# Hybrid delta-rule and retention block on one core: a pause in the background copies and additions of block sums

## The chip, the cores and the metric

The kernel runs on one core of a Trainium2 chip. The metric is the device time of one execution in microseconds (us); of several runs the median counts. The engines of the core are TensorE (PE in the profile, PEld its weight loads), VectorE (DVE), ScalarE (ACT), GpSimd (POOL) and SyncE (SP); each works through its own queue in order. DMA transfers are issued from the queues of SP, ACT and POOL and share the core's 16 DMA engines.

## The reference

One block of a network on 512 rows of 1024 numbers, all in float32:

```python
xn = rmsnorm(x, n_mix_pre)
proj = xn @ w_in                                   # 1024 x 14352, split into q, k, v, z, gates ...
oa = chunk_gated_delta_rule(qa, ka, va, beta, g)   # first branch: 8 heads
ya = (rmsnorm(oa, norm_a) * silu(za)) @ w_br_a
ob = chunk_retention(rotary(qb), rotary(kb), vb)   # second branch: 4 heads
yb = (rmsnorm(ob, norm_b) * silu(gb)) @ w_br_b
mix = (sigmoid(gate_a) * ya + sigmoid(gate_b) * yb) @ w_out
x = x + rmsnorm(mix, n_mix_post)                   # output projection and its norm
hn = rmsnorm(x, n_mlp_pre)
ff = square(relu(hn @ w_up)) @ w_down              # MLP, 4096 wide
return x + rmsnorm(ff, n_mlp_post)
```

## The kernel before

**Products.** Every float32 product is made of three matmuls: operands are split into a high and a low part, and high x high, high x low and low x high are summed in PSUM. Weights come in blocks of 512 KB into a buffer `raw` (L102; two buffers of the pool `ring`, and at most times two more of a second pool, taken in turn); `split_weights` then makes the high part on ScalarE (L145, `whi`, or `keep` where it is to stay) and the low part on VectorE (L146, `wlo`). SyncE's queue issues these loads.

**Block sums.** Several large products use Strassen's scheme with seven instead of eight products of blocks. They need sums of weight blocks, which depend on the weights alone. Class `BlockSums` makes them in device memory, in the background: a sum is made in a tensor `sums`, first by a copy of one block (`copy_block`, two halves of 512 KB, SyncE's queue, L166) and then by additions of other blocks to it, done by the DMA itself (`add_block`, GpSimd's queue, L132). Ten such sets are made: one for z, one for each of the two gates, four for the values and gates of the retention heads, and three for the first three groups of `w_down`. That is 56 copies and 56 additions, 112 jobs. Some additions take another sum as their source (`sums<-sums`) and wait for its landing. The last two sets are those of the second and third group of `w_down`: in the order rows below their tensors are `sums_95` to `sums_98` and `sums_99` to `sums_102`.

**What sets when a job is issued.** `pace` is called behind every load of weights. It has a reckoned time, `spent`: in the first phase that of a planner's clock, later a count that every product advances by its number of columns. When `spent` has reached `queued`, one job is issued behind that load, an addition where its copies are done and the last job was a copy, else a copy, and `queued` grows by `JOB_US`. `queued` starts at `JOBS_FROM`. With 65 and 8.0 the last of the 112 jobs falls due at 65 + 111 * 8 = 953. When a product wants a sum whose jobs are still open, they are all issued at once. The scheduler that orders the instructions of each queue may then move loads among the jobs, but additions keep their program order.

**The stages.** First phase: projections and the delta rule, with chains of small work between the products. Second phase: four retention heads, each a unit of scores, values and gates, and at the end a unit for the second gate (`gate_unit(gb_sums, ...)`), the last unit. Then the last part of `w_br_b` and the mixing of both branches (L1656 to L1666), which ends with transposes into `mix`. After that the pools of the phases are closed and the pool `pm` takes over their memory. Output projection: `row_tiles` with `w_out`, in row tiles of 128 rows; tiles 2 and 3 share the weight blocks as they come, then tile 0, then tile 1, from the kept weights. Each has two PSUM banks of the four named `mm`, so tile 0 takes those of tile 2. After a tile, `mix_done` norms it: `add_normed` squares both halves on ScalarE (L1718) and multiplies them by the broadcast row `post` (`norm_mix_post`) on VectorE (L1729, which also is the last reader of the banks), takes the root (L408 on ScalarE), adds to the residual in `acc` (L1734), norms again with the row `wmlp` (L1759), and TensorE transposes the result (L394) into `hn`. The residual, four loads of x into `acc` (L1738), and the rows `post` and `wmlp` (L1676) are issued on GpSimd's queue, the same as the additions. The next norm's row, `norm_mlp_post`, takes the buffer of `post` when the last tile has used it. Then the MLP: four groups of a product with `w_up` (L92 to L94) and one with `w_down`, the first three by Strassen's scheme (L314) with the block sums.

Of the kernel before, what the change touches and what calls it, by code (L numbers as in the profile page):

```python
# [25 lines left out]
OFF_BA = 6144  # L26
OFF_QB, OFF_KB, OFF_VB, OFF_GB = 6160, 7184, 8208, 10256
OFF_GA, OFF_GBR = 12304, 13328
JOBS_FROM, JOB_US = 65.0, 8.0
SMALL_US, CONV_US, TOK_US, PK_US, INV_US, DB_US = 10.5, 6.5, 2.5, 2.0, 46, 1.2  # L30
VT_US, KS_US, PX_US, PC_US, GATE_US, FEAT_US, INV_PRIO, CONV_PRIO, SMALL_PRIO, KEY_PRIO, DECAY_US, AHEAD, TR_US, REC_PRIO, OUT_PRIO, SUM_PRIO = 2.5, 2.4, 3.5, 2.4, 11.0, 1.0, 0, 600, 800, 600, 20.0, 700, 2.2, 900, 900, 300
DFF = 4096


def shape_constants():
# [27 lines left out]
def hybrid_block_kernel(ctx: ExitStack, tc: tile.TileContext, a: dict, out: bass.AP):  # L63
# [11 lines left out]
    added, spent, queued, clocks = [False], [None], [JOBS_FROM], []  # L75
# [20 lines left out]
    def weights(src, k0, nk, c0, ncols, keep=None, paced=True):  # L96

        n = nk * ncols
        i = next(loads)
        pool, tag = raw_pools[i % len(raw_pools)]  # L100
        raw = pool.tile([P, 1024], F32, tag=tag, name="raw", bufs=2)
        load = nc.sync.dma_start(  # L102
            raw[:, :n].rearrange("p (k c) -> p k c", k=nk),
            src[k0 * P : (k0 + nk) * P, c0 : c0 + ncols].rearrange("(k p) c -> p k c", p=P),
        )
        pace(load)
        with ExitStack() as behind:
            for mark in marks if i < 9 else ():
                behind.enter_context(tc.issue_after(mark.ins))
            return split_weights(raw, n, nk, keep, ahead[0] if i >= 6 else 0)  # L110

    def pace(load):

        if clocks:
            spent[0] = clocks[0].now
        if spent[0] is None:
            return
        if spent[0] < queued[0] or not (trickle or later_adds):
            return
        queued[0] += JOB_US  # L120
        with tc.issue_after(load.ins):
            ready = bool(later_adds) and not any(job[0] is later_adds[0][2] for job in trickle)
            if ready and (added[0] or not trickle):
                add_block()
                added[0] = False
            else:
                copy_block()
                added[0] = True

    def add_block():  # L130
        dst, src, _ = later_adds.pop(0)
        tc.keep_in_program_order(nc.gpsimd.dma_start(dst, src, accum_op=ALU.add))  # L132

    def copy_block():
        sums, part, k = trickle.pop(0)
        sums.copy(part, k)
# [53 lines left out]
    def block_raw(block):  # L190
        n = next(loads)
        pool, tag = raw_pools[n % len(raw_pools)]
        raw = pool.tile([P, 1024], F32, tag=tag, name="raw", bufs=2)
        load = nc.sync.dma_start(raw.rearrange("p (k c) -> p k c", k=2), block)
        pace(load)
        return raw
# [1753 lines left out]
```

## Time and profile before

| | |
|---|---|
| median of 3 runs | 1349.22 us (1349.13, 1349.22, 1353.59) |
| the profiled execution | 1350.82 us, span from first to last instruction 1349.0 us |
| mean granted TensorE clock | 0.996 of full |
| busy: PE, PEld, DVE, ACT, POOL | 98%, 81%, 69%, 47%, 6% of the span |
| DMA | 210.57 MB, 156 GB/s in the mean |

| stretch, us | PE busy | granted clock | DMA share |
|---|---|---|---|
| 0 to 200 | 195.53 | 1.00 | 0.59 |
| 200 to 400 | 197.83 | 1.00 | 0.61 |
| 400 to 600 | 198.47 | 1.00 | 0.71 |
| 600 to 800 | 199.80 | 1.00 | 0.64 |
| 800 to 900 | 99.38 | 1.00 | 0.39 |
| 900 to 950 | 49.22 | 1.00 | 0.68 |
| 950 to 1000 | 43.47 | 0.93 | 0.58 |
| 1000 to 1100 | 99.64 | 1.00 | 0.56 |
| 1100 to 1300 | 200.00 | 1.00 | 0.42 |
| 1300 to 1349 | 41.49 | 0.97 | 0.20 |

The second table is the view of stages, with the four rows from 1000 to 1100 taken together: the busy time of TensorE in each stretch, the share of full speed that its clock was granted, and the mean busy share of the 16 DMA engines. The first phase ends at about 500 us, the second at about 955, the output projection at about 1005, where the products with `w_up` begin. In a row of a timeline the first number is the start in us from the span's beginning, the second the duration, then engine, line, operation, output and input; the brackets hold the idle time before and what ended it. A row of waits reads: who waited, for whom, us in total, how many times, the longest.

### The profile page before, as it was taken

To read this page: it belongs to the slowest core of one execution; us is meant where nothing else is said; L and a number is where in the kernel's file an instruction comes from. 1 tells how busy PE (TensorE), PEld (TensorE's weight loads), DVE (VectorE), ACT (ScalarE), POOL (GpSimd) and SP (SyncE) were. 2 spreads that over 40 slices of the span, in tenths; PEclk is the share of its full clock that TensorE was granted. 3 is DMA by queue.
4 is the path that set the end of the run, shared out by engine and by line. 5 is a ranking of instruction groups with operands and counts; after the bars stand their busy time and mean duration, and the time that the engine had idled before them with its cause. 6 is when DMAs were issued, how large, how long until landed. Compare 5 with 4: busy or idle time off the path is not lost.

```text
span 1349.0 us, 17489 instructions
## 1 busy us (share of the span) xinstructions
PE 1324.8 (98%) x6615; PEld 1097.6 (81%) x6615; DVE 935.2 (69%) x1575; ACT 638.0 (47%) x1126; POOL 79.8 (6%) x83
## 2 busy tenths in 40 slices
PE   9999999999999999999999999999899999999997
PEld 7888888887888878888888888878689888888886
DVE  6889867486566578886676776889475745828535
ACT  5783336554534524544443443445255746346441
POOL 2201100011000001000000000000110000000000
PEclk9999999999999999999999999999999999999999
DMA  6338943467775477886483661656926443625421
GB/s 194 132 105 184 212 105 78 110 166 199 212 163 130 114 198 166 284 252 161 115 230 93 183 193 48 202 161 187 235 85 193 161 151 109 187 95 177 134 79 63
DMA packets 105701, 210.57 MB, mean 156 GB/s; under 512 B 6598, under 2 KB 30320, under 8 KB 105104
## 3 DMA queue, kind: packets, MB, share of 16 engines
q1 hardware_dynamic: 88592, 167.27, 39.2%
q0 software_dynamic: 14704, 35.30, 15.7%
q10 hardware_dynamic: 2320, 6.89, 1.4%
q8 instruction: 52, 0.85, 0.3%
q14 instruction: 33, 0.27, 0.1%
HBM read 205.21 MB, written 62.93 MB: 199 GB/s over the span
## 4 chain that ended last, share of the span: by engine, by line
PE 78%; DVE 8%; DMA 6%; ACT 5%; issue 2%; POOL 0%; DVEq 0%; ACTq 0%; POOLq 0%
PE mm L665 17%; PE mm L314 12%; PE mm L92 10%; PE mm L93 10%; PE mm L94 10%; PE dl L314 9%; PE dl L665 5%; DVE wlo L146 2%; DMA raw<-in_w_in_dram 2%; DMA raw<-sums 1%; DMA post<-in_norm_mix_post_dram 1%; PE tr L674 1%; PE dl L93 1%; ACT whi L145 1%; PE dl L94 1%
## 5 line engine op out<-in xcount | busy, mean ns | idle before, releaser
L145 ACT CAST whi<-raw 128x1024 fp32r<-128x1024 f32 x259 | 272.0, 1052 | 408.9 <-PE mm L93 96.4
L146 DVE TENSOR_TENSOR wlo<-raw,whi 128x1024 fp32r<-128x1024 f32 x259 | 315.4, 1221 | 213.6 <-ACT whi L145 212.3
L665 PE MATMUL mm<-actT,whi 128*128 128x512 f32 x448 | 144.3, 403 | 0.0
L314 PE MATMUL mm<-whi,xsum 128*128 128x512 f32 x384 | 120.5, 390 | 0.0
L94 PE MATMUL mm<-hn,wlo 128*128 128x512 f32 (+1 forms) x288 | 105.4, 366 | 0.0
L93 PE MATMUL mm<-hn,whi 128*128 128x512 f32 (+1 forms) x288 | 105.3, 366 | 0.0
L92 PE MATMUL mm<-hn,whi 128*128 128x512 f32 (+1 forms) x288 | 105.3, 366 | 0.0
L665 PEld LDWEIGHTS mm<-actT,whi 128*128 128x128 f32 x448 | 80.5, 188 | 14.9
L665 PE MATMUL mm<-actT,wlo 128*128 128x512 f32 x224 | 87.7, 392 | 0.0
L314 PEld LDWEIGHTS mm<-whi,xsum 128*128 128x128 f32 x384 | 72.0, 188 | 14.8
L314 PE MATMUL mm<-wlo,xsum 128*128 128x512 f32 x192 | 75.1, 391 | 0.4 <-DVE wlo L146 0.4
L665 PE MATMUL mm<-whi,og 128*128 128x512 f32 x192 | 62.4, 397 | 0.0
L94 PEld LDWEIGHTS mm<-hn,wlo 128*128 128x128 f32 x288 | 54.3, 189 | 8.8
L665 PE MATMUL mm<-whi,actT 128*128 128x512 f32 x176 | 60.4, 405 | 1.0 <-DVE qf L903 1.0
L93 PEld LDWEIGHTS mm<-hn,whi 128*128 128x128 f32 x288 | 54.3, 189 | 8.7
L92 PEld LDWEIGHTS mm<-hn,whi 128*128 128x128 f32 x288 | 54.3, 189 | 8.7
L314 PE MATMUL dl<-whi,ffq 128*128 128x512 f32 x192 | 61.1, 389 | 0.0
L314 PE MATMUL dl<-whi,actT 128*128 128x512 f32 x192 | 61.1, 389 | 0.0
L1782 DVE TENSOR_TENSOR ffq<-r,ffq 128x512 fp32r<-128x512 f32 (+2 forms) x51 | 33.7, 677 | 29.1 <-ACT ffq L1782 29.0
L132 POOL DMA_DIRECT2D sums<-in_w_in_dram x28 | 32.5, 1162 | 355.2 <-DMA sums<-in_w_in_dram 355.2
L92 PE MATMUL mm<-actT,whi 128*128 128x512 f32 x128 | 51.5, 403 | 0.0
L94 PE MATMUL mm<-actT,wlo 128*128 128x512 f32 x128 | 50.8, 397 | 0.0
(394 smaller groups left out, 2894.7 us busy)
## 6 DMA issues: line engine op xcount, KB each, us to landing
raw<-in_w_in_dram SPq DMA_DIRECT2D x95, 512.0 KB, 4.9
raw<-sums SPq DMA_DIRECT2D x56, 512.0 KB, 4.0
raw<-in_w_up_dram SPq DMA_DIRECT2D x36, 512.0 KB, 4.2
sums<-in_w_in_dram SPq DMA_DIRECT2D x32, 512.0 KB, 5.9
sums<-in_w_in_dram POOLq DMA_DIRECT2D x28, 512.0 KB, 7.3
raw<-in_w_down_dram SPq DMA_DIRECT2D x26, 512.0 KB, 3.8
sums<-in_w_down_dram SPq DMA_DIRECT2D x24, 512.0 KB, 6.3
sums<-sums POOLq DMA_DIRECT2D x16, 512.0 KB, 7.9
```

The costliest lines, as they stand in the source:

```text
L92: nc.tensor.matmul(ps, lh, rh, start=first, stop=False)
L93: nc.tensor.matmul(ps, lh, rl, start=False, stop=False)
L94: nc.tensor.matmul(ps, ll, rh, start=False, stop=last)
L132: tc.keep_in_program_order(nc.gpsimd.dma_start(dst, src, accum_op=ALU.add))
L145: nc.scalar.copy(hi[:, :n], raw[:, :n])
L146: nc.vector.tensor_tensor(lo[:, :n], raw[:, :n], hi[:, :n], ALU.subtract)
L314: m = nc.tensor.matmul(pss[t], lhs[i // 2], rhs[i % 2], start=first and k + i == 0, stop=k + i == 5, skip_group_check=not first,)
L665: m = tc.keep_in_program_order(nc.tensor.matmul(*args, **kwargs))
L674: tc.keep_in_program_order(nc.tensor.transpose(ps, src, ident if by is None else by))
L1782: return nc.scalar.copy(dst[0], r), nc.vector.tensor_tensor(dst[1], r, dst[0], ALU.subtract)
```

## The change

Two numbers of the planner change and one rule is added: the jobs start at a reckoned 70 instead of 65 us, fall due every 8.5 instead of 8.0 us, and a job that would fall due between a reckoned 860 and 985 us is put off to 985. By this count 93 jobs fall due before the pause (the 93rd at 70 + 92 * 8.5 = 852) and 19 from 985 on, the last at 985 + 18 * 8.5 = 1138.

```diff
-JOBS_FROM, JOB_US = 65.0, 8.0
+JOBS_FROM, JOB_US = 70.0, 8.5
...
+REST = 860.0, 985.0
...
         queued[0] += JOB_US
+        if REST[0] < queued[0] < REST[1]:
+            queued[0] = REST[1]
         with tc.issue_after(load.ins):
```

The change moves instructions on two queues, SyncE's and GpSimd's; on TensorE, VectorE and ScalarE the same operations stand in the same order as before.

GpSimd's queue around the loads of x and of the norms' rows, before (`acc` is the residual, `post` and `wmlp` the norms' rows, `sums_95` and up the sums for the second and third group of `w_down`):

```order
L132 DMA sums_98<-in_w_down_dram 128x2x512 x2
L1738 DMA acc_624<-in_x_dram 128x1024 x2
L132 DMA sums_99<-in_w_down_dram 128x2x512
L1738 DMA acc_624<-in_x_dram 128x1024
L132 DMA sums_100<-sums_99 128x1024
L132 DMA sums_101<-sums_100 128x1024
L132 DMA sums_99<-in_w_down_dram 128x2x512
L1738 DMA acc_624<-in_x_dram 128x1024
L1676 DMA post_8155<-in_norm_mix_post_dram 128x1024
L1676 DMA wmlp_8157<-in_norm_mlp_pre_dram 128x1024
L132 DMA sums_100<-sums_99 128x1024
L1676 DMA post_8616<-in_norm_mlp_post_dram 128x1024
```

The same place with the change:

```order
L135 DMA sums_97<-sums_96 128x1024
L1741 DMA acc_624<-in_x_dram 128x1024 x4
L1679 DMA post_8144<-in_norm_mix_post_dram 128x1024
L1679 DMA wmlp_8146<-in_norm_mlp_pre_dram 128x1024
L1679 DMA post_8600<-in_norm_mlp_post_dram 128x1024
L135 DMA sums_95<-in_w_down_dram 128x2x512
L135 DMA sums_96<-sums_95 128x1024
L135 DMA sums_97<-sums_96 128x1024
L135 DMA sums_98<-in_w_down_dram 128x2x512 x2
L135 DMA sums_99<-in_w_down_dram 128x2x512
L135 DMA sums_100<-sums_99 128x1024
L135 DMA sums_101<-sums_100 128x1024
```

Between the first load of x and the second row there were four additions and are now none; 13 additions, five of which stood ahead of the first load of x, now follow the third row.

SyncE's queue from the last unit of the second phase to the MLP, before (`raw` are weight loads, `sums<-in_w_down_dram` the copies):

```order
L194 DMA raw<-sums 128x1024
L166 DMA sums<-in_w_down_dram 128x2x512
L194 DMA raw<-in_w_in_dram 128x2x512
L194 DMA raw<-sums 128x1024
L194 DMA raw<-in_w_in_dram 128x2x512
L102 DMA raw<-in_w_br_b_dram 128x1024
L166 DMA sums<-in_w_down_dram 128x2x512
L102 DMA raw<-in_w_br_b_dram 128x1024 x3
L102 DMA raw<-in_w_out_dram 128x1024 x8
L102 DMA raw<-in_w_up_dram 128x2x512 x12
L102 DMA raw<-in_w_down_dram 128x2x512 x2
```

And with the change:

```order
L197 DMA raw<-sums 128x1024
L197 DMA raw<-in_w_in_dram 128x2x512
L103 DMA raw<-in_w_br_b_dram 128x1024 x4
L103 DMA raw<-in_w_out_dram 128x1024 x8
L103 DMA raw<-in_w_up_dram 128x2x512 x11
L169 DMA sums<-in_w_down_dram 128x2x512
L103 DMA raw<-in_w_up_dram 128x2x512
L103 DMA raw<-in_w_down_dram 128x2x512 x2
L169 DMA sums<-in_w_down_dram 128x2x512
L197 DMA raw<-sums 128x1024 x2
```

The copies ended with the loads of `w_br_b` before; now the last six of them, those of the third group's sums except its first tensor, stand among the loads of `w_up` and `w_down` of the first two groups of the MLP.

## Prediction

> **What bounds the kernel now.** The page comes first: TensorE is busy for 98% of the span, so a change that only moves background transfers can give at most the 24 us in which TensorE is not busy, and only where it waits for one of them.
>
> ```profile
> span 1349.0 us, 17489 instructions
> PE 1324.8 (98%) x6615; PEld 1097.6 (81%) x6615; DVE 935.2 (69%) x1575; ACT 638.0 (47%) x1126; POOL 79.8 (6%) x83
> ```
>
> The view of waits for TensorE over the whole run, longest first, then tells where that is. One wait stands far above all others:
>
> ```profile
> PE mm L92 <- DVE nh_v L1720: 6.5, 1, 6.5
> PE warm L472 <- DVE warm L461: 1.2, 1, 1.2
> ```
>
> It happens once, in the output projection (L92 is the matmul helper, L1720 is in the norm that follows each row tile). The table by stages puts it between 970 and 980 us, with TensorE busy for 3.47 us of 10 and DMA engines full (share 1.03), and shows a granted clock of 0.79 in the ten microseconds behind it:
>
> ```profile
> 970.00:980.00 10.00, 3.47 (x14) 2.56 (x13) 1.32 (x4) 2.66 (x5) 0.87 (x1) 0.87 1.03 326
> 980.00:990.00 10.00, 10.00 (x37) 8.00 (x36) 7.04 (x25) 3.26 (x11) 0.00 (x0) 0.79 0.15 33
> ```
>
> The timeline of TensorE there gives the size (start, duration; in brackets the idle time and what ended it):
>
> ```profile
> 970.01 0.39 PE L92 MATMUL mm<-keep,actT 128*128 128x512 f32 x1
> ...
> 972.50 0.39 PE L94 MATMUL mm<-keep,actT 128*128 128x512 f32 x1
> 979.42 0.79 PE L92 MATMUL mm<-whi,actT 128*128 128x512 f32 x1 [6.53 <-DVE nh_v L1720]
> ...
> 984.24 0.39 PE L94 MATMUL mm<-keep,actT 128*128 128x512 f32 x1
> ```
>
> The matmul at 979.42 is the first of row tile 0. It needs a PSUM bank that still holds row tile 2, and VectorE had not read that bank, because its first reader multiplies by the row `post`, which was not there:
>
> ```profile
> 978.68 0.69 DVE L1729 TENSOR_TENSOR fw<-mm,post 128x512 f32<-128x512 f32 x1 [12.98 <-DMA post<-in_norm_mix_post_dram]
> ```
>
> The cause lies one queue further back. GpSimd's queue is in order, and the load of `post` stands in it behind additions of block sums, which wait for one another's landing:
>
> ```profile
> 951.59 0.87 POOL L132 DMA_DIRECT2D sums<-sums  x1 [4.44 <-DMA sums<-in_w_down_dram]
> 960.52 0.82 POOL L132 DMA_DIRECT2D sums<-sums  x1 [8.07 <-DMA sums<-sums]
> 961.78 1.35 POOL L1738 DMA_DIRECT2D acc<-in_x_dram  x1
> 962.40 1.28 POOL L1676 DMA_DIRECT2D post<-in_norm_mix_post_dram  x1
> ...
> 1007.34 0.55 POOL L1676 DMA_DIRECT2D post<-in_norm_mlp_post_dram  x1 [31.56 <-DVE nr_y L413]
> ```
>
> The last of the four loads of x into `acc` goes out at 961.78 and `post` at 962.40, with no wait of their own noted: the queue had only just let them through. And it landed late, since the additions were still moving; the table of DMA issues has the microseconds from issue to landing at the end of each row:
>
> ```profile
> acc<-in_x_dram POOLq DMA_DIRECT2D x4, 512.0 KB, 5.1
> post<-in_norm_mix_post_dram POOLq DMA_DIRECT2D x1, 512.0 KB, 16.2
> wmlp<-in_norm_mlp_pre_dram POOLq DMA_DIRECT2D x1, 512.0 KB, 17.5
> post<-in_norm_mlp_post_dram POOLq DMA_DIRECT2D x1, 512.0 KB, 6.7
> ```
>
> 962.40 + 16.2 = 978.6, which is where VectorE starts.
>
> **The change, part by part.** First, the rest. On GpSimd the four loads into `acc` and the two rows now follow one another with no addition between them (rows in the section on the change); TensorE, VectorE and ScalarE keep their order. What `post` then waits for are the release of `acc` and of the memory that the closed pools held, whose last users the timeline shows:
>
> ```profile
> 953.90 0.68 DVE L1659 SCALAR_TENSOR_TENSOR tb<-tb,acc 128x512 f32<-128x512 f32 x1
> 955.45 0.63 PE L394 MATMUL tr<-cmat,tb 128*128 128x128 f32 x4
> ```
>
> So it goes out at about 955.45 + 0.63 = 956.1 instead of 962.4. VectorE's read takes 0.74 us to release TensorE (978.68 to 979.42), and TensorE wants the bank at 972.50 + 0.23 = 972.73; `post` is in time if it lands by 972.0, within 15.9 us of its issue. The nearest row is the same kind of load in the next norm, 6.7 us, and gives 962.8; the slow one, 16.2 us, would give 972.3 and 0.3 us of wait. I take the 6.7, because the 16.2 belongs to a stretch in which additions filled the engines, and none are left there. The wait ends.
>
> What it is worth: start to start, TensorE loses 979.42 - 972.50 - 0.23 = 6.69 us. Then it runs slow: from 979.42 to 984.24 lie 11 matmuls in 4.82 us, and 11 of the same form take 970.01 to 972.50 = 2.49 us at full clock, so 2.33 us more. Together 9.02 us. The Trainium skill ("TensorE: Matmul & The Clock Gate", Part 1: The HAM clock gate) says that the clock is halved after an idle window of about 3.4 us and comes back after about 3.4 us of work; by it the slow part would cost an estimated 1.7 us instead of 2.33, and the trace agrees in kind, with twice the spacing after 6.5 us of idleness.
>
> What of that is given back. The norm chain could not use its whole lead. ScalarE loads its table for the square root behind the squares, under the wait until now; without the wait this is on the chain:
>
> ```profile
> 972.34 1.28 ACT L408 ACT_TABLE_LOAD   x1
> 980.12 0.20 ACT L408 ACTIVATE nr_y<-nh_v 128x1 f32<-128x1 f32 x1 [6.51 <-DVE nh_v L1721]
> 986.11 1.42 DVE L1759 SCALAR_TENSOR_TENSOR fw<-acc,nr_y,wmlp 128x512 f32<-128x512 f32 x2
> 989.95 0.60 PE L394 MATMUL tr<-cmat,fw 128*128 128x128 f32 x4
> ```
>
> The root moves from 980.12 to the table's end at 973.62, 6.5 us earlier, and the normed row is ready at 986.11 + 1.42 - 6.5 = 981.0. TensorE's transposes of it move by 9.02, from 989.95 to 980.9; the first four need only the first half of the row. That is just met, and as the later tiles follow the same chain with a few tenths of slack, I give back 0.3 us. 9.02 - 0.3 = **8.7 us gained**.
>
> Second, the 19 jobs that come later: 6 copies on SyncE's queue and 13 additions on GpSimd's, 8 of which stood in this stretch before, 5 ahead of it. In the first feature product of the MLP a weight block lasts 24 matmuls, and the stage rows show 44 matmuls in 5 us, so 2.7 us a block:
>
> ```profile
> 1010.00:1015.00 5.00, 5.00 (x44) 5.00 (x43) 4.55 (x8) 3.36 (x8) 1.13 (x1) 1.00 0.87 204
> 1020.00:1025.00 5.00, 5.00 (x44) 5.00 (x44) 2.45 (x2) 2.64 (x4) 0.00 (x0) 1.00 1.06 329
> 1008.43 2.70 POOL L132 DMA_DIRECT2D sums<-in_w_down_dram  x2
> q1 hardware_dynamic: 88592, 167.27, 39.2%
> q0 software_dynamic: 14704, 35.30, 15.7%
> ```
>
> By the two queue rows 512 KB occupy all engines for 0.392 * 1349 * 0.524 / 167.27 = 1.66 us as a load and 0.157 * 1349 * 0.524 / 35.30 = 3.14 us on GpSimd's queue. The additions start behind the MLP's `post`, at 1007.34 - 8.7 = 998.6, and the first three wait for one another, so in the 22 us of the eight blocks fall some 3 * 3.14 + 8 * 1.66 = 22.7 us of traffic: full, but before, too, the row at 1007.34 and two additions at 1008.43 ran beside these blocks, with shares of 0.87 to 1.06, and TensorE was busy 5.00 us of 5. So I take 0. From above: the next four additions (12.6 us of engine time) come in a burst at about 1018; were the loads held up that long, the four raw buffers (two pools of two) still cover 4 * 2.7 = 10.9 us of it at best and nothing at worst, so 1.7 to 12.6 us. The Trainium skill ("DMA: Bandwidth & Descriptors", Queues, rings and completion order) has the engines take turns between queue rows by packets, so that additions slow the loads that run beside them; that speaks against the change, and the rows above say that it has not yet cost TensorE anything.
>
> Are the sums late? The second group's first block sum was fetched at 1115.14, the third group's at 1196.74:
>
> ```profile
> 1115.14 5.58 SPq L194 DMA_DIRECT2D raw<-sums  x2
> 1196.74 5.58 SPq L194 DMA_DIRECT2D raw<-sums  x2
> 1077.08 21.90 SPq L102 DMA_DIRECT2D raw<-in_w_up_dram  x8
> sums<-in_w_down_dram POOLq DMA_DIRECT2D x12, 512.0 KB, 11.2
> raw<-in_w_up_dram SPq DMA_DIRECT2D x36, 512.0 KB, 4.2
> ```
>
> Less 8.7 these are 1106 and 1188. Three chained additions of 11.2 us from 998.6 end at 1032; the last of the third group go out behind copies that stand between the eight weight loads of 1077 to 1099, and end before 1130. Both have over 50 us in hand: cost 0.
>
> Third, the interval. Up to the rest, 93 jobs run at 8.5 instead of 8.0 us of reckoned time, and every sum is still copied long before its use. TensorE is idle for 5.6 us of these 795:
>
> ```profile
> 65.00:860.00 795.00, 789.42 (x4023) 652.56 (x4022) 579.00 (x1014) 362.29 (x658) 55.43 (x52) 1.00 0.62 160
> ```
>
> That is the most that it could give. A copy can as well fall ahead of another load than before; for a loss I bound it by the same 5.6 us, and take 0, as the longest waits there are for VectorE and ScalarE.
>
> The sum: the profiled execution took 1350.82 us for a span of 1349.0; it becomes 1340.3 of span and 1342.1. The median of the runs is 1349.22, so 1349.22 - 8.7 = **1340.5 us**.
>
> **Rivals.** *The row is still late.* With the 17.5 us of `wmlp` from 956.1, `post` lands at 973.6, 1.6 us too late; the wait stays too short to bring back the slow clock, if the rule above holds, and 1342.1 comes out. For it: weight loads share the engines at that time. Against it: the four loads into `acc` on the same queue took 5.1 us in the median. Chance 0.10.
>
> *Crowding in the MLP.* The burst of additions eats half of the buffers' lead: 12.6 - 5.4 = 7.2 us at most, about 4 in the middle, 1344.5. For it: shares of 1.06 already. Against it: TensorE's full stages beside them. Chance 0.16.
>
> *Starved loads, slower.* At the start of the second half of the first group, about 1018, loads find no buffer lead and TensorE stops for the whole 12.6 us, in two pieces that each bring the slow clock, 2 * 2.33 more: 17.3 - 8.7 = 8.6 us slower, 1357.8. It decides if loads of `w_up` take longer than 10.9 us to land. Against it: 4.2 us is their median now. Chance 0.05.
>
> *No effect.* Another transfer lets VectorE go at the same time, or the rest is filled otherwise: 1349. But ScalarE's squares were done when its table load began at 972.34, the loads into `acc` are ahead of `post`, and the order shows the rest to be empty. Chance 0.04.
>
> **How the numbers follow.** The forecast keeps 0.65, with a range of its own of 1338.5 to 1343. A measurement of this kernel can tell about 0.5%, here 6.7 us, from no change; faster means under 1342.5. The forecast gives 0.61 of that and the late row 0.06, crowding 0.05: 0.72. Slower is the starved case and a little of the interval's unknown: 0.06. The rest, 0.22, is no change. For 8 in 10 the range reaches over the late row and the middle of crowding: 1338.5 to 1346.5.
>
> **What would show it.** In the profile of the changed kernel `post` goes out near 956 and lands before 972; the wait of L92 for L1720 is gone; the granted clock reads 1.00 from 950 to 1000; the table load stands between the squares and the root; additions stand at 999 and later, and TensorE is full from 1000 to 1100. Idle time of L92 to L94 for `whi` or `wlo` after 1000, or `post` landing after 972, would make the prediction wrong, as would new waits of over 3 us before 940.

## The result and the profile after

| | before | after |
|---|---|---|
| median of 5 runs each, us | 1349.91 (1349.13 to 1353.59) | 1340.97 (1338.08 to 1342.55) |
| span of the profiled execution, us | 1349.0 | 1339.2 |
| first matmul of the output projection starts at, us | 950.27 | 949.27 |
| from there to the end of the span, us | 398.7 | 389.9 |

The ratio of the times is 0.9924, 95% interval 0.9904 to 0.9945: faster by 0.55% to 0.96%. The last row of the table is the difference of the two rows above it. It will serve as the yardstick of the experiments, because what lies ahead of the projection varies between executions of the same code: in five profiles in which the program is the changed kernel up to there, the first matmul of the projection starts between 946.2 and 950.6 us. The yardstick is not exact either: a second profile of the changed kernel has 391.0 instead of 389.9, so differences of about 1 us in it say little. Every distance, landing and wait below comes from one profiled execution of its kernel.

The code has moved by three lines: L92 to L94 are now L93 to L95, L394 is L397, L1729 is L1732. The busy line of the page of after:

```profile
span 1339.2 us, 17492 instructions
PE 1323.0 (99%) x6615; PEld 1095.8 (82%) x6615; DVE 935.8 (70%) x1575; ACT 637.6 (48%) x1126; POOL 78.1 (6%) x83
```

TensorE does as many matmuls in about the same busy time (1324.8 before). The span lost 9.8 us: 8.0 of idle time and 1.8 of busy time, since a slow matmul counts as busy. In the view of waits of after, TensorE alone, from 940 us to the end, the row of 6.5 us is gone and one row is left:

```profile
PE tr L397 <- DVE fw L1762: 0.3, 1, 0.3
```

The table by stages of after, for the places that the prediction named:

```profile
970.00:980.00 10.00, 10.00 (x47) 8.23 (x46) 7.14 (x23) 5.79 (x16) 0.00 (x0) 1.00 0.00 0
980.00:990.00 10.00, 10.00 (x54) 8.47 (x53) 8.34 (x27) 5.58 (x15) 0.00 (x0) 1.00 0.00 0
...
1060.00:1080.00 20.00, 20.00 (x89) 16.30 (x88) 12.96 (x15) 8.77 (x11) 0.85 (x1) 1.00 1.03 258
```

From 970 to 990 TensorE is full at a granted clock of 1.00, and the DMA engines, full from 970 to 980 before, have nothing to do. The traffic went to the MLP: in the last row they are full (1.03), in this profile without a loss on TensorE. GpSimd's timeline of after:

```profile
945.56 0.53 POOL L1741 DMA_DIRECT2D acc<-in_x_dram  x1 [4.17 <-DVE tb L1662]
953.88 0.53 POOL L1741 DMA_DIRECT2D acc<-in_x_dram  x1 [7.79 <-DVE tb L1662]
955.63 0.53 POOL L1679 DMA_DIRECT2D post<-in_norm_mix_post_dram  x1 [1.23 <-DMA raw<-in_w_out_dram]
...
997.27 0.53 POOL L1679 DMA_DIRECT2D post<-in_norm_mlp_post_dram  x1 [40.59 <-DVE nr_y L416]
997.79 1.25 POOL L135 DMA_DIRECT2D sums<-in_w_down_dram  x1
```

Between the last loads of x and the rows no addition stands (the first two loads, at 936.02 and 940.85, have none behind them either), and the brackets name what ended each wait: VectorE's last reads of the old memory, and for `post` a load of `w_out`. `post` leaves at 955.63 instead of 962.40. The table of DMA issues of after:

```profile
post<-in_norm_mix_post_dram POOLq DMA_DIRECT2D x1, 512.0 KB, 8.3
...
raw<-in_w_up_dram SPq DMA_DIRECT2D x36, 512.0 KB, 5.3
```

It lands at 955.63 + 8.3 = 963.9. So VectorE's first read of the bank waits for something else now, the squares on ScalarE (timeline of VectorE, then of ScalarE):

```profile
970.59 0.69 DVE L1732 TENSOR_TENSOR fw<-mm,post 128x512 f32<-128x512 f32 x1 [7.88 <-ACT junk L1721]
```

```profile
971.32 1.28 ACT L411 ACT_TABLE_LOAD   x1
972.61 0.20 ACT L411 ACTIVATE nr_y<-nh_v 128x1 f32<-128x1 f32 x1
```

and TensorE goes from tile 2 and 3 to tile 0 without a gap (timeline of TensorE):

```profile
971.48 0.39 PE L95 MATMUL mm<-keep,actT 128*128 128x512 f32 x1
971.71 0.39 PE L93 MATMUL mm<-whi,actT 128*128 128x512 f32 x1
...
974.20 0.39 PE L95 MATMUL mm<-keep,actT 128*128 128x512 f32 x1
...
979.88 0.60 PE L397 MATMUL tr<-cmat,fw 128*128 128x128 f32 x4
```

These are the last matmul of the two tiles, the first and the twelfth of tile 0, and the transposes of the normed row. Before they stood at 972.50, 979.42, 984.24 and 989.95.

### The profile page after: what moved, and what is told of

Its sections match the earlier page's. It is cut to its first block, busy times and chain, and to the rows that moved or that the text cites. A ratio compares the mean times of both kernels' runs of the same rounds, so it can differ in the third digit from the quotient of the medians.

```text
span 1339.2 us, 17492 instructions
## 1 busy us (share of the span) xinstructions
PE 1323.0 (99%) x6615; PEld 1095.8 (82%) x6615; DVE 935.8 (70%) x1575; ACT 637.6 (48%) x1126; POOL 78.1 (6%) x83
## 4 chain that ended last, share of the span: by engine, by line
PE 83%; DVE 7%; ACT 5%; DMA 4%; issue 1%; DVEq 0%; ACTq 0%; SPq 0%
PE mm L668 17%; PE mm L317 12%; PE mm L95 11%; PE mm L94 11%; PE mm L93 11%; PE dl L317 8%; PE dl L668 5%; DVE wlo L149 2%; DMA raw<-in_w_in_dram 2%; PE dl L93 1%; PE dl L95 1%; PE dl L94 1%; DMA raw<-sums 1%; PE tr L397 1%; PE tr L677 1%
## 5 line engine op out<-in xcount | busy, mean ns | idle before, releaser
L95 PE MATMUL mm<-hn,wlo 128*128 128x512 f32 (+1 forms) x288 | 105.4, 366 | 0.0
L94 PE MATMUL mm<-hn,whi 128*128 128x512 f32 (+1 forms) x288 | 105.3, 366 | 0.0
L93 PE MATMUL mm<-hn,whi 128*128 128x512 f32 (+1 forms) x288 | 105.3, 366 | 0.0
L95 PEld LDWEIGHTS mm<-hn,wlo 128*128 128x128 f32 x288 | 54.3, 189 | 8.8
L94 PEld LDWEIGHTS mm<-hn,whi 128*128 128x128 f32 x288 | 54.3, 189 | 8.7
L93 PEld LDWEIGHTS mm<-hn,whi 128*128 128x128 f32 x288 | 54.3, 189 | 8.7
L93 PE MATMUL mm<-actT,whi 128*128 128x512 f32 x128 | 51.5, 403 | 0.0
L95 PE MATMUL mm<-actT,wlo 128*128 128x512 f32 x128 | 50.8, 397 | 0.0
```

Source lines behind the costliest of these rows:

```text
L93: nc.tensor.matmul(ps, lh, rh, start=first, stop=False)
L94: nc.tensor.matmul(ps, lh, rl, start=False, stop=False)
L95: nc.tensor.matmul(ps, ll, rh, start=False, stop=last)
```

## Experiments

Each experiment starts from the kernel before or from the changed one, as its diff shows. "Distance" is the last row of the table above: from the first matmul of the output projection to the end (398.7 us before, 389.9 after).

**Pause or interval?** The change has two parts that can both move the additions. First the numbers alone, without the pause:

```diff
-JOBS_FROM, JOB_US = 65.0, 8.0
+JOBS_FROM, JOB_US = 70.0, 8.5
```

> Jobs from 70 every 8.5, without the pause. In GpSimd's queue the row post then stands behind only two additions that come after the first load of x (one onto sums_97, one onto sums_98), and neither has to wait for another's landing, since their sources were finished long before. Theory 1 (the row stood behind additions that wait for one another): post goes out by 957, lands before 971, the wait of tile 0 for its bank is gone, and the time is 8 to 9 us below the kernel before, ratio 0.993 to 0.995, although there is no pause. Theory 2 (the pause, that is less traffic around the output projection, brings the gain): post lands after 975, TensorE still waits 5 to 7 us, ratio 0.999 to 1.001.

Measured: 1340.0 us (1338.69 to 1341.81, 5 runs), ratio 0.9932, interval 0.9915 to 0.995; distance 389.9. GpSimd's timeline of this kernel shows how:

```profile
943.45 0.90 POOL L132 DMA_DIRECT2D sums<-sums  x1
944.01 1.54 POOL L132 DMA_DIRECT2D sums<-in_w_down_dram  x1
946.61 0.58 POOL L1738 DMA_DIRECT2D acc<-in_x_dram  x1 [1.06 <-DVE tb L1659]
...
956.49 0.53 POOL L1676 DMA_DIRECT2D post<-in_norm_mix_post_dram  x1 [3.93 <-PE tr L394]
```

Two additions still stand among the loads of x, but neither waits for another's landing, and nothing is held up; `post` lands 8.3 us after its issue. Then the pause alone, with 65 and 8.0:

```diff
+REST = 860.0, 985.0
...
+        if REST[0] < queued[0] < REST[1]:
+            queued[0] = REST[1]
```

> The pause alone, jobs from 65 every 8.0. No addition stands between the loads of x and the rows. Theory 1 and theory 2 both: the wait for post is gone, ratio 0.993 to 0.995. Theory 3 (part of the gain comes from the longer interval in the first two phases): 1 to 3 us less gain than the whole change, ratio 0.995 to 0.997, and TensorE reaches the output projection about 1 us later than with the whole change.

Measured: 1340.49 us (1338.18 to 1342.98, 6 runs), ratio 0.9932, interval 0.9914 to 0.9951; distance 389.7. Either part does the whole work, and the two together (the change, once more beside other kernels) no more than each:

> The changed kernel itself, once more on the chip of the two kernels beside it: 1338 to 1342.5 us, no wait of L95 for the norm. If either of the other two stands below it by more than 2 us in the median, a version without a pause beats it.

Measured: 1339.78 us (1338.28 to 1341.39, 6 runs), ratio 0.9912, interval 0.9894 to 0.9931; distance 391.0. Of the 1.1 us above the first profile's 389.9, TensorE idles 0.7 between 1060 and 1080, where it waits for split weights in the MLP (of which below):

```profile
1060.00:1080.00 20.00, 19.30 (x84) 15.34 (x83) 11.87 (x13) 8.11 (x9) 0.85 (x1) 1.00 0.99 253
```

The times of the three kernels agree. So it is not the pause as such, and not the interval as such: both clear the place ahead of `post` of additions that wait for each other.

**The queue or the traffic?** In the next kernel the additions stay where they were before; only the rows `post` and `wmlp` change their queue, from GpSimd's to SyncE's.

```diff
-        def broadcast_row(vec, tag):
+        def broadcast_row(vec, tag, eng=nc.gpsimd):
...
-            rows_in.append(nc.gpsimd.dma_start(w, vec.partition_broadcast(P)))
+            rows_in.append(eng.dma_start(w, vec.partition_broadcast(P)))
...
-        wpost = broadcast_row(a["norm_mix_post"][0], "post")
-        wmlp = broadcast_row(a["norm_mlp_pre"][0], "wmlp")
+        wpost = broadcast_row(a["norm_mix_post"][0], "post", nc.sync)
+        wmlp = broadcast_row(a["norm_mlp_pre"][0], "wmlp", nc.sync)
```

> The kernel before, with all its jobs where they were, but post and wmlp are loaded from SyncE's queue. Theory 1: post goes out at about 956 and, among the additions' traffic, lands 7 to 16 us later, so between 963 and 972; TensorE waits 0 to 1 us, the clock stays at 1.00 or nearly, ratio 0.993 to 0.996. Theory 2 (traffic): it lands near 978 as before, wait of 5 to 7 us, ratio 0.999 to 1.001.

Measured: 1342.53 us (1339.24 to 1348.93, 12 runs), ratio 0.9951, interval 0.9934 to 0.9967; distance 391.5. SyncE's timeline of this kernel, its DMA issue of `post`, GpSimd's timeline, and its view of waits for TensorE from 940 us:

```profile
955.51 0.33 SPq L1676 DMA_DIRECT2D post<-in_norm_mix_post_dram  x1
...
956.39 0.46 SPq L102 DMA_DIRECT2D raw<-in_w_out_dram  x1
```

```profile
post<-in_norm_mix_post_dram SPq DMA_DIRECT2D x1, 512.0 KB, 8.3
```

```profile
962.77 0.82 POOL L132 DMA_DIRECT2D sums<-sums  x1 [10.03 <-DMA sums<-sums]
```

```profile
PE mm L93 <- DVE keep L146: 0.8, 1, 0.8
PE mm L92 <- ACT keep L145: 0.6, 1, 0.6
```

The row goes out at 955.51, and on GpSimd's queue additions go on at 951.88, 962.77 and 963.32, with the fourth load of x held up until 964.03 as before. The row lands in 8.3 us all the same, and the wait for the norm is gone. The 1.4 us of other waits are the price of the new place: the rows are issued ahead of the last load of `w_out`, whose split TensorE then waits for. So the additions hurt by standing ahead of the row in its queue. The addition of 951.88, which lands only at about 962.7, runs beside the row and does no harm; those of 962.77 and 963.32 go out as the row lands, at 963.8, so what they would do beside it is not shown.

The opposite: a chain put back. With 70 and 9.5 and no pause, the jobs reach the projection later, and a chain of three additions stands ahead of the fourth load of x and of `post`.

```diff
-JOBS_FROM, JOB_US = 65.0, 8.0
+JOBS_FROM, JOB_US = 70.0, 9.5
```

> No pause, jobs from 70 every 9.5, so fewer transfers than in the changed kernel up to the output projection, but by this count three additions that wait for one another (onto sums_95, 96 and 97) stand between the loads of x, ahead of post. Theory 1 (the chain in GpSimd's queue sets the time): the first goes out at about 942, the next two after 8 to 9 us each, the fourth load of x and post at about 961 to 963; post lands 8 to 16 us later, at 969 to 979. TensorE waits 0 to 7 us for the bank, and the time lies between the changed kernel's and that before, ratio 0.994 to 1.000, most likely 0.997. Theory 3 (a longer interval is what helps): ratio 0.993 or lower, as with 8.5.

GpSimd's timeline of this kernel, its DMA issue of `post`, and its waits of TensorE:

```profile
940.80 1.24 POOL L132 DMA_DIRECT2D sums<-in_w_down_dram  x1
...
948.76 0.86 POOL L132 DMA_DIRECT2D sums<-sums  x1 [3.47 <-DMA sums<-in_w_down_dram]
956.65 0.81 POOL L132 DMA_DIRECT2D sums<-sums  x1 [7.03 <-DMA sums<-sums]
957.20 0.84 POOL L1738 DMA_DIRECT2D acc<-in_x_dram  x1
958.10 0.56 POOL L1676 DMA_DIRECT2D post<-in_norm_mix_post_dram  x1
```

```profile
post<-in_norm_mix_post_dram POOLq DMA_DIRECT2D x1, 512.0 KB, 13.2
```

```profile
PE dl L314 <- DVE wlo L146: 1.1, 2, 0.8
PE mm L92 <- DVE nh_v L1720: 1.1, 1, 1.1
PE dl L314 <- ACT whi L145: 0.9, 1, 0.9
```

Measured: 1346.42 us (1341.93 to 1355.88, 12 runs), ratio 0.9976, interval 0.9959 to 0.9994; distance 394.1. The wait for the norm is back, but with 1.1 us: here the chain began earlier, and `post` was held only until 958.10. Still it landed 13.2 us later, against 8.3 without a chain. That gives the lateness of before two parts: in the kernel before `post` was issued 5.8 us later than in the changed one (counted from the first matmul of the projection: 12.13 against 6.36) and took 7.9 us longer to land (16.2 against 8.3). By these numbers neither part alone would have cost much: an estimate for the kernel before is 962.40 + 8.3 = 970.7 with the late issue alone, in time for the 972.0 of the prediction, and 956.6 + 16.2 = 972.8 with the slow landing alone, 0.8 us late. The other 2.0 us of waits in this kernel are in the MLP, of which below.

**A late row without any addition.** If the lateness of the row is all that counts, the changed kernel must fall back when the row is late for another reason. In three kernels GpSimd fills the row's buffer with zeros several times (1 us each) before the load; nothing else is changed, and the extra fills are overwritten. The row `wmlp` now goes out ahead of `post`, behind the first fill.

```diff
-        def broadcast_row(vec, tag):
+        def broadcast_row(vec, tag, fills=0):
...
+            for _ in range(fills):
+                nc.gpsimd.memset(w, 0.0)
...
-        wpost = broadcast_row(a["norm_mix_post"][0], "post")
+        wpost = broadcast_row(a["norm_mix_post"][0], "post", 15)
```

Fifteen fills:

> The changed kernel, but GpSimd first fills the buffer of post 15 times, about 0.95 us each, so that the row goes out at about 970 instead of 955.6; no addition is near. Theory 1: it lands 6 to 8.5 us later, at 976 to 979, and the old picture returns without any addition: TensorE waits 5 to 7 us for the bank, then some 4 us of matmuls at half the clock, and the span is 7 to 9.5 us over that of the changed kernel. Theory 2: no traffic, so no loss beyond 1 us.

Thirteen:

> As the run with 15 fills, with 13: post goes out 1.9 us earlier. That run's row landed 3.5 us after its issue and TensorE was idle 3.5 us. Theory 1: TensorE idle 1.3 to 2.0 us for the bank. If the clock falls only after some 3.4 us of idleness, the granted clock stays at 1.00 and the span is 1 to 2.5 us over the changed kernel's; if it falls after any wait, 10 matmuls run at half the clock again.

Twenty:

> As the run with 15 fills, with 20: post goes out 4.8 us later than there, with no addition near. Theory 1: TensorE idle 8.0 to 8.6 us for the bank, then 7 to 11 matmuls at half the clock (1.4 to 2.4 us), span 1347 to 1351, the time of the kernel before. Theory 2 (traffic): the time of the changed kernel.

One execution of each was profiled. The first matmul of tile 0 in the three timelines of TensorE, with 13, 15 and 20 fills (L1734 is the multiplication by `post` there):

```profile
972.83 0.50 PE L93 MATMUL mm<-whi,actT 128*128 128x512 f32 x1 [1.84 <-DVE fw L1734]
```

```profile
972.25 0.50 PE L93 MATMUL mm<-whi,actT 128*128 128x512 f32 x1 [3.46 <-DVE fw L1734]
```

```profile
982.15 0.80 PE L93 MATMUL mm<-whi,actT 128*128 128x512 f32 x1 [8.92 <-DVE fw L1734]
```

| fills | `post` issued, lands after | TensorE idle | slow matmuls behind it | distance | one time |
|---|---|---|---|---|---|
| 13 | 968.13, 3.9 | 1.84 | none | 393.7 | 1343.85 |
| 15 | 967.94, 3.5 | 3.46 | 7, from the seventh on | 396.9 | 1344.85 |
| 20 | 977.45, 3.9 | 8.92 | 11, from the first on | 401.9 | 1354.22 |

A slow matmul is one that takes 0.43 instead of 0.23 us to the next. With 20 fills the picture of before is there again, wait and slow clock, with no addition within 30 us. The size in the first of these kernels was missed: with nothing else moving, the row landed within 3.5 us of its issue, so 15 fills made TensorE idle for 3.46 us only, and the span is 3.9 us over the changed kernel's, not 7 to 9.5. That is why the other two were run. They came out near the forecasts but a little beyond them: with 13 fills the idle time and the clock are as expected and the span is 2.9 us over instead of 1 to 2.5, 0.8 of it a wait in the MLP; with 20 the idle time is 8.92 instead of 8.0 to 8.6 and the span 1352.5 instead of 1347 to 1351.

**Does the traffic in the MLP cost anything?** First more of it. The pause is made longer, so that 37 instead of 19 jobs come behind it (75 fall due before, the 75th at 70 + 74 * 8.5 = 699; the trace, too, has 22 additions and 15 copies there, and the 38 of the expectation is one too many):

```diff
-REST = 860.0, 985.0
+REST = 700.0, 985.0
```

> The pause from a reckoned 700 instead of 860, so that 38 jobs instead of 19 come after it, the last additions of the first group's sums among them. Theory 1: the norm's wait stays gone. The moved traffic costs TensorE nothing as long as sums are in time: the first group's first sum is wanted at about 1024, and its last of four chained additions from 997 lands at 1024 to 1032, so TensorE waits 0 to 8 us there, and for the second group's not at all. Ratio 0.993 to 0.999. Rival (transfers crowd the weight loads of the MLP, as weighed in the prediction): waits for whi or wlo of w_up spread over 1000 to 1100, over 3 us in all, ratio above 0.996.

Measured: 1345.03 us (1342.35 to 1347.14, 8 runs), ratio 0.9959, interval 0.9942 to 0.9976; distance 396.4. Rows of this kernel: two stages, a DMA issue, ScalarE's waits for loads of `w_up`, and ScalarE and TensorE in the first of the two stages.

```profile
1060.00:1080.00 20.00, 17.90 (x71) 14.08 (x70) 10.71 (x13) 6.64 (x8) 0.85 (x1) 0.91 1.01 248
...
1150.00:1200.00 50.00, 48.09 (x211) 39.22 (x210) 23.62 (x29) 18.11 (x24) 5.34 (x6) 1.00 0.88 233
```

```profile
raw<-in_w_up_dram SPq DMA_DIRECT2D x36, 512.0 KB, 9.0
```

```profile
ACT whi L148 <- DMA raw<-in_w_up_dram: 24.5, 8, 7.4
```

```profile
1073.14 1.04 ACT L148 CAST whi<-raw 128x1024 fp32r<-128x1024 f32 x1 [4.88 <-DMA raw<-in_w_down_dram]
```

```profile
1074.23 0.50 PE L317 MATMUL dl<-whi,ffq 128*128 128x512 f32 x1 [1.34 <-ACT whi L148]
1075.49 0.51 PE L317 MATMUL dl<-wlo,ffq 128*128 128x512 f32 x1 [0.76 <-DVE wlo L149]
```

The loads of `w_up` take 9.0 us in the median, against 5.3 with the change and 4.2 before. ScalarE, which splits the blocks, waits for late loads, of `w_down` in the first of the two stages and of `w_up` in the second, and TensorE loses 2.1 us in one and 1.9 in the other; the first loss is followed by the slow clock. So the crowding that the prediction held as a rival exists, and it does not begin only above 19 jobs. With the changed kernel's 19 jobs TensorE waits for split weights in the same part of the MLP, between 1060 and 1080 us, in three of five profiles: 0.7 us in the repeated change, 0.8 with 13 and 0.6 with 15 fills, none in the first profile or with 20 fills. The kernel with 9.5 has 17 jobs in the MLP (13 additions, 4 copies) and waits 2.0 us there. The number alone does not set the cost; what does is not shown. The Trainium skill ("DMA: Bandwidth & Descriptors", Queues, rings and completion order) has each DMA engine take turns between the queue rows packet by packet; the slower loads beside more additions agree with that.

Then none of it. With an interval of 7.0 and no pause all 112 jobs are due before the projection:

```diff
-JOBS_FROM, JOB_US = 65.0, 8.0
+JOBS_FROM, JOB_US = 65.0, 7.0
```

> The kernel before with jobs from 65 every 7.0 us and no pause, so that all 112 jobs fall due by a reckoned 842 and no addition is left for the output projection or the MLP. Queue theory (the row must not stand behind chained additions; where else the additions run does not matter): `post` goes out at 954 to 957, lands within 9 us, L92 does not wait for the norm, the granted clock is 1.00 from 960 to 990, and the time is 1338 to 1342 us, as with the change. Rival (denser jobs crowd the weight loads of the second phase, whose DMA share rises): TensorE loses 2 us or more between 500 and 940 against the change and the time is 1343 us or more. Rival (the MLP beside additions costs the change something): the MLP without any addition gains against it, and the time is under 1338 us.

Measured: 1360.42 us (1358.62 to 1362.51, 6 runs), ratio 1.0065, interval 1.0046 to 1.0084, slower than before. But the distance is 389.7 us, the same as with the change. So by the distance the 19 jobs cost the changed kernel 0.2 us at most in its first profile and 1.3 at most in the repeat (391.0), and all the loss here lies ahead of the projection, whose first matmul starts at 967.13 instead of 949.27. The view of waits of this kernel, TensorE:

```profile
PE dl L92 <- ACT osq L1567: 4.5, 1, 4.5
PE mm L314 <- DVE wlo L146: 3.6, 4, 1.6
PE mm L314 <- ACT whi L145: 2.5, 2, 2.0
```

One more kernel was to show that an addition which waits for nothing does no harm ahead of `post`. It met the same wait for L1567 (`osq`) as the kernel with 7.0:

```diff
-JOBS_FROM, JOB_US = 65.0, 8.0
+JOBS_FROM, JOB_US = 70.0, 8.25
```

> The kernel before with jobs from 70 every 8.25 us and no pause: two additions that wait for nothing stand among the loads of x, one more than before at that point but none that waits for another's landing. Queue theory: `post` goes out by 958, lands within 10 us, no wait of L92 for the norm, 1339 to 1342 us. If any addition near the row is enough to delay it (traffic, not the queue): landing 13 us or more, a wait of 3 us or more, 1345 us or more.

Measured: 1345.54 us (1343.21 to 1348.45, 7 runs), ratio 0.9959, interval 0.9936 to 0.9982. Its distance is 389.6 us, `post` goes out at 961.81, 6.35 us after the projection's first matmul (6.36 with the change), lands within 7.7 us, and no wait for the norm is left. So the queue theory holds in its place and the expected time does not: the first matmul of the projection starts at 955.46. Where the 6.2 us went is told by the timelines of three engines and the chain of waits of this kernel, shown in the order of the story (GpSimd, the chain with start, duration and work, ScalarE, TensorE):

```profile
775.76 0.85 POOL L132 DMA_DIRECT2D sums<-sums  x1 [12.31 <-DMA sums<-in_w_down_dram]
785.60 0.81 POOL L132 DMA_DIRECT2D sums<-sums  x1 [8.98 <-DMA sums<-sums]
```

```profile
773.08 13.16 DMA raw<-in_w_in_dram
```

```profile
786.34 1.04 ACT L145 CAST whi<-raw 128x1024 fp32r<-128x1024 f32 x1 [4.55 <-DMA raw<-in_w_in_dram]
...
788.34 0.57 ACT L1567 ACTIVATE osq<-dl 128x512 f32<-128x512 f32 x1
```

```profile
789.06 0.80 PE L92 MATMUL dl<-vr,s 128*128 128x512 f32 x1 [4.68 <-ACT osq L1567]
```

In a unit of a retention head a load of weights takes 13.16 us beside a chain of additions. ScalarE waits for it with the split L145, and behind that split in its queue stands L1567, which reads a PSUM bank (`dl`) that TensorE needs. TensorE idles for 4.68 us and then runs some ten matmuls at half clock, about 2 us more. With 8.0 and 8.5 the additions fall elsewhere, and this wait is 0.2 us at most. That a shift of the chain is all that brings it about was not tried apart.

## Why the prediction held, point by point

**The time.** Forecast were 1340.5 us, 8.7 less than before; measured were 1340.97, and 8.9 less by the medians of five runs.

**The bound and its cause** were right, but for one thing: the 24 us of idle time are not all that can be won, since slow matmuls count as busy. The prediction itself added 2.33 us for them, and the busy time fell by 1.8. The one long wait of TensorE was for the norm, through the row `post`, through GpSimd's queue. It goes when the additions go (the change, its two parts alone), it goes when the row leaves that queue (rows on SyncE), and it comes back with a late row alone (20 fills).

**The issue and the landing.** Forecast were 956.1 and 6.7 us; measured 955.63 and 8.3. That the issue came 0.5 us early is the projection's doing, which began 1.0 us earlier: counted from its first matmul, 5.8 were forecast and 6.4 measured. The prediction named the last transposes as what lets the row go; they end at 955.09 (954.46 + 0.63), and the profile names a load of `w_out` in their place. The row of the next norm was a slightly low price, and the reason for taking it was not right: the DMA engines are as full while the row moves (shares 0.98 and 1.02 in the two stretches of 5 us from 955 to 965) as they were before, and it lands faster all the same. The margin covered the difference: VectorE begins to read at 970.59, when ScalarE's squares are done, 6.7 us after the landing at 963.9.

**What the wait was worth.** Forecast 9.02 us. The twelfth matmul of tile 0 moved from 984.24 to 974.20, 10.04 us, and the last one ahead of the tile from 972.50 to 971.48, 1.02 us; the difference is 9.02. The step had counted the slow clock as 2.33 of it, and it belongs there: without the wait the clock stays at 1.00.

**What was given back.** The table load came onto the norm's chain where it was forecast, with the root directly behind it (972.61). At the transposes it cost nothing: they moved by 10.07 us, as much as the matmuls. By the distance 398.7 - 389.9 = 8.8 us were won; by the repeated profile, with its 391.0, it is 7.7. So the step is right to about 1 us, and that 8.8 lies within 0.1 of the 8.7 of the forecast is luck.

**The 19 later jobs** were taken to cost 0, because TensorE had been full beside shares of 0.87 to 1.06. In the first profile they cost nothing; in the repeated one TensorE waits 0.7 us for split weights, so the term is small but not 0. With 37 jobs the loads of `w_up` took 9.0 us, near the 10.9 us of cover that four buffers were reckoned to give at best, and the distance grew by 6.5 us. The sums themselves were in time, as forecast: the additions start at 997.79, the last goes out at 1099.61, and in that profile TensorE has no wait behind 940 us but one of 0.3 for the norm.

**The interval** was priced at 0 and came out at 0 (the pause alone and the change have the same distance, 389.7 and 389.9, and the same time within the spread), but the reason given for it was weak. The idle time that TensorE had in these 795 us bounds what an interval can win, not what it can lose. The bound for a loss was put at the same 5.6 us; an interval of 8.25 moved the projection's start by 6.2 us against the change, and one of 7.0 by 17.9.

**The rivals.** The late row fell with the landing at 963.9, no effect with the time, and starved loads with the distance of 389.9 us beside 389.7 without any addition in the MLP. Crowding fell at the 4 us that it was priced at; a small form of it, 0 to 0.8 us of waits with the 19 jobs, is there.

**The remaining 1.0 us**, ahead of the projection, was not forecast, and nothing speaks for an effect of the change: five profiles of the same code spread over 4.5 us there.

## What to carry to other kernels

In a queue that works in order, a background job that waits for another job's landing is a barrier for every load behind it: look for what stands behind such jobs, and issue what is needed at a fixed time ahead of them or from a queue without them. Background transfers have to be placed by what they stand before, not by an even interval: of five intervals between 7.0 and 9.5 us, two that looked alike to the planner (8.25 and 8.5) differed by 5.5 us (1345.54 and 1340.0), and with the slower one a chain runs beside a load on which a PSUM bank's release depends; that this is the whole cause was read from its rows and not tried apart. To tell a cause from the spread of the runs, measure from a mark right ahead of the place that was changed.

## What was not expected of the hardware

**The same row landed in 3.5 to 16.2 us.** The 512 KB took 3.5 to 3.9 us alone (the late rows), 8.3 beside weight loads on another queue, 8.3 on SyncE's queue beside an addition, and 13.2 and 16.2 behind additions on GpSimd's queue. That additions slow it on their own queue above all is what these five numbers suggest; no run changes that alone.

**The clock's answer to a pause.** Idle times of 1.1 and 1.84 us left the granted clock at 1.00; 3.46 us brought half the clock, but only from the seventh matmul on, 1.6 us after work had begun again, for seven matmuls; 4.68, 6.53 and 8.92 us brought it at once or nearly so, for ten to eleven matmuls. The length of one wait does not decide it alone: in the kernel with 37 later jobs waits of 1.34 and 0.76 us with a single matmul between them (1074.23 and 1075.49) were followed by about seven matmuls at half the clock. The Trainium skill ("TensorE: Matmul & The Clock Gate", Part 1: The HAM clock gate) has the clock halved after an idle window of about 3.4 us that runs freely. The single waits agree with it in size, the two short ones do not fit it as it stands; the delay after 3.46 us is something that a window which does not start with the idleness can bring, but no run here shows the window itself.
